# A sum of h split later on ScalarE, and two gate row copies moved to VectorE

## Chip, cores and metric

One core of one Trainium2 chip runs the whole program. The metric is the device time of one execution in microseconds, the median of three runs. TensorE does the matmuls, ScalarE (ACT) and VectorE (DVE) read their results and prepare their operands, SyncE (SP) and GpSimd (POOL) issue most of the transfers.

## What is computed

One decoder layer over 512 tokens of width 1024, in float32. What matters here is the head of it: the normalised input h is multiplied by the columns of one wide weight, in pieces.

```python
h = rmsnorm(x, norm_mix_g[i])
proj = h @ w_in[i]
qk_ml, v_ml, o_ml, if_pre, q_sw, k_sw, v_sw, g_a, g_b = jnp.split(proj, split_idx, axis=-1)
...
gates = (if_pre + b_if[i].astype(if_pre.dtype)).astype(jnp.float32)
ig = gates[..., :ML_HEADS]
lf = jax.nn.log_sigmoid(gates[..., ML_HEADS:])
h_ml = mlstm_chunkwise(q_ml, k_ml, v_ml.reshape(B, S, ML_HEADS, ML_DV), ig, lf)
```

Behind it come the mLSTM and the sliding-window attention, their two branch projections and the output projection, an MLP of width 4096, a gated per-layer embedding and a last norm.

## The kernel before

**Operands.** Every float32 operand of a product is split in a high part (rounded by ScalarE) and a low part (the rest, by VectorE), and each product takes three matmuls: high by high, high by low, low by high. `split` (L219) does so for a weight of 128x1024: the cast makes `wh`, the subtraction `wl`. There are four buffers of each (WB), and `load_w` (L243) is what loads and splits one. A weight that is loaded stands in `wr` or, from a scratch buffer, in `wq`.

**Seven products.** A projection over two halves of the tokens and two of the columns is done with seven block products in place of eight (`seven`, L646). These take, on the side of h, besides three blocks of h itself the four sums S1 to S4 of blocks; on the side of the weight they take the four blocks b11, b12, b21, b22, and sums of them that VectorE makes in place. Each block comes as two halves of 128x1024 in `by_tokens` (L711), and each half gives 12 matmuls of 512 columns. The products in order: p1 (A11), the one that ends in c11 (A12), u2 (S2 with the first form of b11), p5 (S1 with its second form), the one with S3, the one with S4 that ends in c12, and the one with A22.

**The sums of h.** S1 and S2 are made early. S3 and S4 are made in `late_sums` (L638), which `seven` calls in its first use (the v projection) behind the low part of b21. Each sum is split by `split_by_transfer` (L229): for each half a cast on ScalarE, a negated copy on ScalarE, and a transfer on POOL that adds the sum to that copy. So a sum costs four ScalarE instructions of 128x512 and two transfers; all of these write tiles named `hS`. The sums s1 to s4 lie in two scratch buffers of tag pT, which later hold weights of the gate projection b (`quads` of L269, named `wq`, loaded from in_w_gb by SP).

**The gates.** The pre-activations of the gates are turned into rows by eight small transposes into one bank pair, `pgi` and `pgf` (L763 to L767); behind the v projection the 4x512 rows are copied out as `ig` and `fg` (L777, L778), and `gates` (L799) works on them, beginning with `lf` on VectorE.

**Order.** In this part no order is written out by hand: instructions of an engine stand in a queue that is set when the program is built, by place in the program but with later work taken forward where earlier work isn't ready by the builder's own reckoning. `tc.issue_after(ins)` puts what is traced inside it, on the engine of `ins`, behind `ins`. Each engine runs its queue in order, and so does SP with its loads.

**Names.** `psa`, `pst`, `psg` are PSUM tiles; `p` is a product kept in SBUF and added to; `vm` and `vl` are the high and low part of v (L748), `vs` is a value of the attention, used far later (L1041).

Of the kernel before, what the change touches and what calls it, by code (L numbers as in the profile page):

```python
# [117 lines left out]
def block_kernel(  # L118
# [34 lines left out]
    V, A, G, T, L = [Turns(tc, e, fixed) for e in (nc.vector, nc.scalar, nc.gpsimd, nc.tensor, nc.sync)]  # L153
# [43 lines left out]
    def act_hl(n="s"):  # L197
        return [act_r(n), act_r(n)]
# [15 lines left out]
    def r32(t):  # L214
        return t.bitcast(F32)

    last_low = [None]

    def split(dst, src, scale=None):  # L219

        if scale is None:
            A.copy(dst[0], src)
            last_low[0] = V.tensor_sub(dst[1], src, r32(dst[0]))
        else:
            done = A.activation(dst[0], src, AF.Copy, scale=scale)
            V.scalar_tensor_tensor(dst[1], src, scale, r32(dst[0]), ALU.mult, ALU.subtract)
            return done

    def split_by_transfer(dst, src):  # L229

        A.copy(dst[0], src)
        A.activation(dst[1], src, AF.Copy, scale=-1.0)
        return nc.gpsimd.dma_start(out=r32(dst[1]), in_=src, accum_op=ALU.add)
# [9 lines left out]
    def load_w(src, n, dims, raw=None, cast=False, behind=None):  # L243

        if raw is None:
            raw = load_raw(src, n)
        parts = [wp.tile([P, 1024], F32R, tag=t, bufs=WB, name=nm(t))[:, :n] for t in ("wh", "wl")]
        if cast:
            nc.gpsimd.dma_start(out=parts[0], in_=src)
            with tc.issue_after(behind.ins) if behind else ExitStack():  # L250
                last_low[0] = V.tensor_sub(parts[1], raw[:, :n], r32(parts[0]))
        else:
            split(parts, raw[:, :n])
        return [q.rearrange("p (k c) -> p k c", k=dims) for q in parts]
# [317 lines left out]
    def hf_part(tok, par):  # L572

        return [hf[t + (2 if tok == 1 else 0)].rearrange("p (k two) c -> p k two c", two=2)[:, :, par - 1, :] for t in range(2)]
# [3 lines left out]
    def h_sum(name, a, b, op):  # L578
        t = sp.tile([P, 4, 256], F32, tag="pT", bufs=2, name=nm(name))
        halves = [t[:, :, :P], t[:, :, P:]]  # L580
        for i in range(2):
            V.tensor_tensor(halves[i], a[i], b[i], op)
        return t, halves
# [3 lines left out]
    def h_split(t):  # L587
        f = []
        for kh in range(2):
            hl = [q.rearrange("p (k c) -> p k c", k=2) for q in act_hl("hS")]  # L590
            summed[0] = split_by_transfer(hl, t[:, 2 * kh : 2 * kh + 2, :])
            f += [[q[:, k, :] for q in hl] for k in range(2)]
        return f
# [42 lines left out]
    S3, S4 = [], []  # L636

    def late_sums():  # L638
        s4, _ = h_sum("s4", hf_part(1, 2), s2h, ALU.subtract)
        s3, _ = h_sum("s3", hf_part(1, 1), hf_part(2, 1), ALU.subtract)  # L640
        S3.extend(h_split(s3))
        S4.extend(h_split(s4))

    ADDED = {"c11": "p1", "c22": "p5", "c12": "u2"}

    def seven(form, prod, X, Y, Z, b, post, own_first=False, sums_late=False, swapped=False, behind=None):  # L646

        b11, b12, b21, b22 = b  # L650
        n = range(len(b11))
        for i in n:
            prod(X, A11, form(b11[i]), i, True)
        post("p1", X)

        def weight_sums():
            for i in n:
                V.tensor_sub(b12[i], b22[i], b12[i])
                V.tensor_add(b11[i], b12[i], b11[i])

        if sums_late:
            w21 = [form(t) for t in b21]
            with tc.issue_after(last_low[0].ins):
                weight_sums()
        else:
            with tc.issue_after(behind.ins) if behind else ExitStack():
                weight_sums()
        for i in n:
            prod(Y, A12, w21[i] if sums_late else form(b21[i]), i, True, True)
        own = last_mm[0].ins  # L670
        if own_first:
            with tc.issue_after(last_low[0].ins):
                late_sums()
        post("c11", Y)
        for i in n:
            w = form(b11[i]) if sums_late else None
            with tc.issue_after(last_low[0].ins) if sums_late else ExitStack():
                V.tensor_sub(b21[i], b21[i], b11[i])
            w = w or form(b11[i])
            with tc.issue_after(own) if own_first else ExitStack():  # L680
                prod(X, S2, w, i, False)
            V.tensor_sub(b11[i], b22[i], b11[i])
        post("u2", X)
        if swapped:
            for i in n:
                prod(X, S3, form(b12[i]), i, False)
            post("u3", X)
        for i in n:
            prod(Z, S1, form(b11[i]), i, True)
        if swapped:  # L690
            post("c22", Z)
        else:
            post("p5", Z)
            for i in n:
                prod(X, S3, form(b12[i]), i, False)
            post("c22", X)
        rest = [("c12", Z, S4, b22), ("c21", X, A22, b21)]
        for what, ps, f, b in rest[::-1] if swapped else rest:
            for i in n:
                prod(ps, f, form(b[i]), i, False, True)  # L700
            post(what, ps)
# [9 lines left out]
    def by_tokens(w, post, own_first=False, sums_late=False):  # L711

        raws = quads(w, ["wr", "wr", "lm", "lm", "wr", "wr", "lm", "lm"])
        b = ps_a()
        X, Y, Z = [b[:, :512], b[:, 512:]], [ps_t(), ps_t()], [ps_g(), ps_g()]

        def prod(ps, f, w, kh, first, last=False):
            for t in range(2):
                ops = []
                for k in range(2):  # L720
                    ops += pairs([h[:, t * P : (t + 1) * P] for h in f[2 * kh + k]], [h[:, k, :] for h in w])
                chain(ps[t], ops, first and kh == 0, last and kh == 1, True)

        seven(lambda r: load_w(None, 1024, 2, r), prod, X, Y, Z, [raws[2 * i : 2 * i + 2] for i in range(4)], post, own_first, sums_late, behind=gate_in if own_first else None)
# [39 lines left out]
    pgi, pgf = pg[:, :512], pg[:, 512:]  # L764
# [7 lines left out]
    def row(n):  # L772
        return c1.tile([P, 512], F32, tag="row", bufs=NH, name=nm(n))

    ig = row("ig")[:4, :]
    fg = row("fg")[:4, :]
    A.copy(ig, pgi[:4, :])  # L777
    A.copy(fg, pgf[:4, :])  # L778
    god = dp.tile([P, NH, NT, DV], F32, name="god")

    def put_o(m, nh, ps, k):
# [64 lines left out]
    def by_features(blocks, tags, done, beside={}, swapped=False):  # L846
# [23 lines left out]
        def post(what, ps):  # L870
# [9 lines left out]
            for work in beside.pop(what, ()):  # L880
                work()

        seven(lambda r: load_w(None, 1024, 4, r), prod, X, Y, Z, [raws[i : i + 1] for i in range(4)], post, swapped=swapped, behind=added_last.get("c22") if swapped else None)

    def gate_proj(wd, beside={}):
# [129 lines left out]
    def swa_out(kp, ns):  # L1015

        terms = {n: swa_turn(kp, n) for n in ns}
        sums = {n: swa_sum(kp, terms[n]) for n in reversed(ns)}
        for n in ns:
            for g in range(4):  # L1020
                if n == 0:
                    yb[kp * 4 + g] = act_hl("yb")
                split([t[:, n * P : (n + 1) * P] for t in yb[kp * 4 + g]], sums[n][:, g * P : (g + 1) * P])
# [41 lines left out]
    def qk_parts(h):  # L1065
        for i in (h, 4 + h):
            hl = spare()
            split(hl, qk[i])
            qk[i] = hl
# [331 lines left out]
    A11, A22, A12, S3, S2, S1, S4 = range(7)  # L1401
# [48 lines left out]
    def form(user, dims, deps):  # L1450

        parts = []

        def high():
            parts.extend(wp.tile([P, 1024], F32R, tag=t, bufs=WB, name=nm(t)) for t in ("wh", "wl"))
            return [A.copy(parts[0], slots[user])]

        def low():
            return [V.tensor_sub(parts[1], slots[user], r32(parts[0]))]

        free = [forms[-WB]["use"]] if len(forms) >= WB else []
        h = plan.add("ACT", HI, high, deps + free + [w["hi"] for w in forms[-1:]])
        lo = plan.add("DVE", LO, low, [h] + free)
        w = {"hi": h, "lo": lo, "get": lambda: [q.rearrange("p (k c) -> p k c", k=dims) for q in parts]}
        forms.append(w)
        return w
# [618 lines left out]
```

## Time and profile before

| | |
|---|---|
| median of 3 runs | 859.73 us (859.72 to 860.01) |
| the profiled execution | 859.77 us |
| its span, first to last instruction | 858.0 us |
| TensorE matmuls busy | 848.6 us (99%) |
| VectorE busy | 722.4 us (84%) |
| ScalarE busy | 532.7 us (62%) |
| mean granted TensorE clock | 0.997 |

The profile is of one execution; its times run from the first instruction. Matmul records overlap, since they are pipelined, so the sum of the busy shares says less than the distance from one start to the next. Idle time of an engine counts only where TensorE waits in the end.

### The profile page before, as it was taken

How to read it: one execution, taken by the hardware profiler on the slowest of the kernel's cores; microseconds unless marked ns; L12 is line 12 of the kernel's file. 1: busy time of each engine (PE TensorE's matmuls, PEld its weight loads, DVE VectorE, ACT ScalarE, POOL GpSimd, SP SyncE). 2: the span in 40 equal slices, each digit the busy share in tenths (PEclk: the TensorE clock that was granted, in tenths of full speed). 3: DMA queues.
4: the chain of work that ended last, by engine and by line, in shares of the span. 5: the costliest groups of instructions: out<-in, count | busy, mean ns of one | idle time of the engine just before them, and what ended most of it. 6: DMA issues, size and time to landing. Idle time of an engine off the chain costs nothing.

```text
span 858.0 us, 12975 instructions
## 1 busy us (share of the span) xinstructions
PE 848.6 (99%) x4936; PEld 740.8 (86%) x4936; DVE 722.4 (84%) x1058; ACT 532.7 (62%) x923; POOL 59.3 (7%) x92
## 2 busy tenths in 40 slices
PE   9999999999999999999999999999999999999996
PEld 8878789999987778888888888899889989988886
DVE  6898979777799978777997799879988997999656
ACT  7786657556587758854353685458537744764743
POOL 2221111000000000000020000000000000010000
PEclk9999999999999999999999999999999999999998
DMA  7777235444421147468234271753455364634302
GB/s 294 216 190 283 91 131 199 148 147 147 149 73 50 50 138 254 167 221 297 104 61 133 96 226 49 217 133 117 98 173 147 113 178 130 170 102 134 134 1 99
DMA packets 37536, 125.71 MB, mean 147 GB/s; under 512 B 5213, under 2 KB 5213, under 8 KB 37474
## 3 DMA queue, kind: packets, MB, share of 16 engines
q1 hardware_dynamic: 28146, 95.77, 32.2%
q0 software_dynamic: 9184, 28.85, 13.9%
q8 instruction: 39, 0.64, 0.3%
q10 hardware_dynamic: 144, 0.26, 0.1%
q14 instruction: 23, 0.19, 0.1%
HBM read 106.51 MB, written 11.54 MB: 138 GB/s over the span
## 4 chain that ended last, share of the span: by engine, by line
PE 92%; DVE 5%; ACT 2%; issue 1%; DVEq 0%; ACTq 0%
PE psg L109 38%; PE psp L109 34%; PE psa L109 15%; PE pst L109 5%; DVE wl L109 1%; DVE wr L109 1%; ACT wh L109 1%; DVE wq L109 1%; DVE qs L109 1%; ACT hS L109 0%; ACT hf L109 0%; DVE s L109 0%; DVE kl L109 0%; DVE lm L109 0%; DVE pT L109 0%
## 5 line engine op out<-in xcount | busy, mean ns | idle before, releaser
L109 ACT CAST wh<-wr 128x1024 fp32r<-128x1024 f32 (+1 forms) x151 | 156.7, 1049 | 146.6 <-DVE wr L109 54.7
L109 DVE TENSOR_TENSOR wl<-wr,wh 128x1024 fp32r<-128x1024 f32 (+1 forms) x160 | 192.8, 1213 | 45.3 <-ACT wh L109 41.7
L109 PE MATMUL psp<-x,wh 128*128 128x256 f32 x672 | 121.3, 283 | 0.0
L109 PE MATMUL psp<-wh,uf 128*128 128x512 f32 x336 | 106.2, 390 | 0.0
L109 PEld LDWEIGHTS psp<-x,wh 128*128 128x128 f32 x672 | 105.0, 192 | 0.3
L109 PE MATMUL psp<-x,wl 128*128 128x256 f32 x336 | 95.1, 283 | 0.0
L109 PEld LDWEIGHTS psp<-wh,uf 128*128 128x128 f32 x336 | 63.1, 188 | 14.2 <-issue 1.2
L109 ACT CAST wh<-wd 128x1024 fp32r<-128x1024 f32 x45 | 47.2, 1049 | 33.0 <-PE psp L109 27.7
L109 PE MATMUL psp<-wl,uf 128*128 128x512 f32 x168 | 65.5, 390 | 0.0
L109 PEld LDWEIGHTS psp<-x,wl 128*128 128x128 f32 x336 | 64.5, 192 | 0.0
L109 PE MATMUL psg<-h,wh 128*128 128x512 f32 x192 | 60.9, 396 | 0.0
L109 DVE TENSOR_TENSOR wl<-wd,wh 128x1024 fp32r<-128x1024 f32 x45 | 54.7, 1218 | 3.1 <-ACT wh L109 3.1
L109 DVE TENSOR_TENSOR wr<-wr,wr 128x1024 f32<-128x1024 f32 x35 | 42.7, 1221 | 1.7 <-DMA wr<-in_w_gb 0.6
L109 PEld LDWEIGHTS psg<-h,wh 128*128 128x128 f32 x192 | 35.1, 188 | 9.0 <-issue 2.4
L109 DVE TENSOR_TENSOR uf<-F,uf 128x512 fp32r<-128x512 f32 (+3 forms) x36 | 34.9, 982 | 6.4 <-ACT uf L109 6.4
L109 PE MATMUL psg<-x,wh 128*128 128x512 f32 x128 | 39.5, 390 | 0.0
L109 PE MATMUL psg<-h,wl 128*128 128x512 f32 x96 | 37.7, 393 | 0.0
L109 PEld LDWEIGHTS psp<-wl,uf 128*128 128x128 f32 x168 | 31.5, 188 | 6.7 <-DVE wl L109 0.3
L109 PE MATMUL psg<-wh,uf 128*128 128x512 f32 x112 | 36.5, 389 | 0.0
L109 ACT CAST uf<-F 128x512 fp32r<-128x512 f32 (+3 forms) x36 | 30.7, 856 | 7.5 <-DVE F L109 7.1
L109 PE MATMUL psg<-ya,wh 128*128 128x512 f32 x112 | 34.8, 391 | 0.0
L109 DVE SCALAR_TENSOR_TENSOR xk<-psp,r,xk 128x512 f32<-128x512 f32 x42 | 30.4, 745 | 4.8 <-PE psp L109 4.7
(355 smaller groups left out, 2090.0 us busy)
## 6 DMA issues: line engine op xcount, KB each, us to landing
wr<-in_w_down SPq DMA_DIRECT2D x16, 512.0 KB, 4.7
wd<-in_w_down SPq DMA_DIRECT2D x16, 512.0 KB, 4.3
wr<-in_w_upb SPq DMA_DIRECT2D x12, 512.0 KB, 4.0
wd<-in_w_upb SPq DMA_DIRECT2D x12, 512.0 KB, 4.6
gd<-gr POOLq DMA_DIRECT2D x8, 512.0 KB, 3.0
wr<-in_w_qkml SPq DMA_DIRECT2D x8, 512.0 KB, 3.3
wr<-in_w_b SPq DMA_DIRECT2D x8, 512.0 KB, 3.4
wh<-in_w_b POOLq DMA_DIRECT2D x8, 512.0 KB, 3.9
```

Of the source, the lines that this page charges most:

```text
L109: ins = op(*args, **kw)
```

## The change

Three things are done. `split` keeps the last cast it issued. `late_sums` makes s3 and s4 and splits s3 as before, but hands s4 back; `seven` splits s4 behind its loop over u2, and on ScalarE behind the last cast issued there, which is the one of the second half of b11. And the two copies of gate rows are issued by VectorE.

```diff
@@ split
-    last_low = [None]
+    last_low, last_cast = [None], [None]
...
         if scale is None:
-            A.copy(dst[0], src)
+            last_cast[0] = A.copy(dst[0], src)
             last_low[0] = V.tensor_sub(dst[1], src, r32(dst[0]))
@@ late_sums
         S3.extend(h_split(s3))
-        S4.extend(h_split(s4))
+        return s4
@@ seven
         if own_first:
             with tc.issue_after(last_low[0].ins):
-                late_sums()
+                s4 = late_sums()
         post("c11", Y)
...
             V.tensor_sub(b11[i], b22[i], b11[i])
+        if own_first:
+            with tc.issue_after(last_cast[0].ins):
+                S4.extend(h_split(s4))
         post("u2", X)
@@ behind the v projection
-    A.copy(ig, pgi[:4, :])
-    A.copy(fg, pgf[:4, :])
+    V.tensor_copy(ig, pgi[:4, :])
+    V.tensor_copy(fg, pgf[:4, :])
```

## Rows read from the trace of the kernel before

**Rows 1.** The page: busy time and share of each engine; the last chain by engine.
```profile
PE 848.6 (99%) x4936; PEld 740.8 (86%) x4936; DVE 722.4 (84%) x1058; ACT 532.7 (62%) x923; POOL 59.3 (7%) x92
...
PE 92%; DVE 5%; ACT 2%; issue 1%; DVEq 0%; ACTq 0%
```

**Rows 2.** Waits of TensorE's matmuls, whole span: who for whom, us, times, longest.
```profile
PE psg L109 <- DVE zero L109: 1.1, 1, 1.1
PE psa L109 <- DVE wl L109: 0.5, 1, 0.5
```

**Rows 3.** Windows: stretch, length, busy us of each engine, clock, DMA share, GB/s.
```profile
56.75:63.03 6.28, 5.78 (x26) 4.43 (x24) 5.61 (x7) 6.25 (x9) 3.20 (x4) 1.00 1.06 205
63.03:68.60 5.57, 5.57 (x25) 4.42 (x24) 4.64 (x5) 5.54 (x8) 0.00 (x0) 1.00 0.98 338
68.60:74.04 5.44, 5.44 (x25) 4.50 (x24) 4.60 (x8) 3.48 (x5) 0.00 (x0) 1.00 1.00 393
```

**Rows 4.** Timeline of TensorE's weight loads, 56 to 66: start, us, what, idle before.
```profile
60.36 0.19 PEld L109 LDWEIGHTS psa<-wl,hS 128*128 128x128 f32 x1 [0.92 <-DVE wl L109]
...
63.23 0.19 PEld L109 LDWEIGHTS psg<-wl,hS 128*128 128x128 f32 x1 [0.24 <-DVE wl L109]
```

**Rows 5.** Timeline of ScalarE, 46 to 60.
```profile
46.52 0.57 ACT L109 COPY ig<-psa 4x512 f32<-4x512 f32 x1
...
48.65 0.58 ACT L109 CAST qs<-psg 64x512 fp32r<-64x512 f32 x1 [1.09 <-DVE qs L109]
...
53.31 0.63 ACT L109 CAST hS<-s 128x512 fp32r<-128x512 f32 x1
...
55.40 0.62 ACT L109 CAST hS<-s 128x512 fp32r<-128x512 f32 x1
...
57.48 0.62 ACT L109 CAST vm<-p 128x512 fp32r<-128x512 f32 x1
57.99 1.05 ACT L109 CAST wh<-wr 128x1024 fp32r<-128x1024 f32 x1
...
59.47 1.05 ACT L109 CAST wh<-wr 128x1024 fp32r<-128x1024 f32 x1
```

**Rows 6.** Timeline of VectorE, 55 to 63.
```profile
55.32 0.67 DVE L109 SCALAR_TENSOR_TENSOR lf<-fg 4x512 f32<-4x512 f32 x1
55.92 0.41 DVE L109 TENSOR_TENSOR vs<-vs,vs 128x256 f32<-128x256 f32 x1
56.35 1.36 DVE L109 TENSOR_TENSOR p<-pst,p 128x512 f32<-128x512 f32 x2
58.13 0.69 DVE L109 TENSOR_TENSOR vl<-p,vm 128x512 fp32r<-128x512 f32 x1 [0.42 <-ACT vm L109]
59.08 1.23 DVE L109 TENSOR_TENSOR wl<-wr,wh 128x1024 fp32r<-128x1024 f32 x1 [0.25 <-ACT wh L109]
...
60.82 1.22 DVE L109 TENSOR_TENSOR wr<-wq,wr 128x1024 f32<-128x1024 f32 x1
61.96 1.22 DVE L109 TENSOR_TENSOR wl<-wr,wh 128x1024 fp32r<-128x1024 f32 x1
```

**Rows 7.** Waits of SP's queue, 40 to 90.
```profile
SPq L276 <- DMA hS<-s: 12.0, 2, 9.6
```

**Rows 8.** The tile wq, 40 to 90: durations in ns, first and last start.
```profile
L276 SPq DMA_DIRECT2D wq<-in_w_gb x2: 333/334/334, 59.7 to 62.6; - x2
```

**Rows 9.** Timelines of SP, TensorE and ScalarE, 63 to 78.
```profile
63.20 1.81 SPq L276 DMA_DIRECT2D wr<-in_w_o x2
...
74.04 0.39 PE L109 MATMUL psg<-wh,hS 128*128 128x512 f32 x1
...
77.00 1.05 ACT L109 CAST wh<-wr 128x1024 fp32r<-128x1024 f32 x1 [0.67 <-ACT vm L109]
```

**Rows 10.** The tile hS: its transfers from issue to landing.
```profile
DMA to landing us min/median/max: 3.2/4.0/6.5
```

**Rows 11.** The tile gc: the copies from PSUM on VectorE, durations in ns.
```profile
L109 DVE COPY gc<-pst x5: 154/160/161, 150.7 to 151.0; 128x16 f32<-128x16 f32 x2, 128x4 f32<-128x4 f32 x1, 128x8 f32<-128x8 f32 x1, 128x12 f32<-128x12 f32 x1
```

## The prediction

> **What bounds the kernel now.** I read four views, from wide to narrow. First the busy times and the chain that ended last: TensorE matmuls fill 99% of the span and 92% of the chain [rows 1], so an edit on ScalarE or VectorE can only matter where TensorE waits for one of them. Second, TensorE's own waits, the whole span through: beside 1.1 us at the very start there is one of any size, 0.5 us in a product into psa for a low weight part `wl` written by VectorE [rows 2]. Third, the stretch around that wait: from 56.75 to 68.60 TensorE runs the 24 matmuls of u2 and the 24 of p5 of the first seven products (the v projection). The 24 matmuls of the next product take 5.44 us [rows 3]; those of u2 take 6.28 and those of p5 5.57. So the stretch loses 0.84 + 0.13 = **0.97 us**, and that is all that this change can win near its place. The granted clock is 1.00 in all three windows, the upper of the two levels (2.4 GHz), so no clock is to be won. Fourth, what TensorE was late for: the weight load of u2's second half waits 0.92 us and that of p5's first half 0.24 us, both for a `wl` of VectorE [rows 4].
>
> Why are these late? ScalarE runs the eight instructions of the third and fourth sum of h (hS) back to back from 53.31; those of the fourth begin at 55.40, then comes one `vm`, and only at 57.99 the rounding `wh` of u2's second half [rows 5]. VectorE can make its `wl` from 59.08 on, and it ends at 60.31 [rows 6]. The `wl` of p5's first half has another cause: its `wh` starts at 59.47 and takes 1.05, so it is there at 60.52 [rows 5], but VectorE comes to it only at 61.96, behind `vl` and the sum of a weight (wr from wq and wr, at 60.82) [rows 6]. So the first wait is ScalarE's queue, the second VectorE's own queue.
>
> **The change part by part.** Part one, the four instructions of the fourth sum go behind the cast `wh` of u2's second half. The third sum still runs 53.31 to 55.40. The cast then takes 55.40 to 56.45 instead of 57.99 to 59.04 [rows 5]: 2.6 us sooner, 2.1 by the four instructions and 0.5 by the `vm`, which isn't ready at 55.40, since its `p` is added on VectorE from 56.35 on [rows 6]. ScalarE's work until the next cast (p5's first half) is the same sum in another order, so that cast still ends near 60.5.
>
> What is moved with the fourth sum: its two transfers on POOL and what waits for them. Four instructions from 56.45 end at 58.5, where they now end near 57.5, so the last transfer is issued about 1.0 us later. The load of a weight of the next stage but one (in_w_gb) into the scratch buffer that the sum frees is issued on SP at 62.6, after SP waited 12.0 us in two waits for such transfers [rows 7, 8]; behind it in SP's queue stand the loads of w_o, the first at 63.20 [rows 9]. They go perhaps 0.5 us later, and ScalarE first rounds a piece of w_o at 77.00, 13.8 us after that issue [rows 9]: free. TensorE reads the fourth sum from 74.04 on [rows 9]; issued near 59 and with a landing of at most 6.5 us [rows 10] it is there by 65.5: free as well, by 8.5 us. Were that cover gone, each us late would be a us of TensorE.
>
> Part two, the two copies of gate rows. On ScalarE they take 0.57 us each, two in a row from 46.52 on (the first stands in the rows), and behind them ScalarE idles 1.09 us for VectorE's `qs` [rows 5]: taking them out gives nothing. On VectorE they are new. No row shows a 4x512 copy from PSUM there. Below it lies the small copy from PSUM, 0.16 us for 4 to 16 columns [rows 11]; above it the 4x512 operation with one tensor, 0.67 us [rows 6]. I take 0.60, the start-to-start distance of that operation and the next (55.32 to 55.92), since the width is equal. So VectorE gets 2 x 0.60 = **1.20 us** more (0.32 to 1.34), in the very stretch in which it makes the two late `wl`. As the rows of their consumer show (`lf` at 55.32 and `vs` at 55.92, both far later in the program, run in a hole ahead of `p`), work that nobody needs soon goes where VectorE would wait. I expect the copies in that same hole, since `lf` depends on one of them, and `lf` and `vs` (55.32 to 56.35, 1.03 us) [rows 6] pushed out of it, behind the weights.
>
> The Trainium skill speaks against part two: Perfetto Trace Analysis, section Optimizing Scalar/DVE Operations, gives about 125 ns of access overhead for DVE on PSUM against 51 ns for Scalar, and advises to move work from a saturated DVE to Scalar, not the other way. By its two figures the move costs an estimated 2 x 0.07 = 0.15 us of engine time more than it saves; the rows agree on the load (VectorE 5.61 busy of 6.28 us in u2's window [rows 3]), and the rule's result is the second rival below.
>
> The sum on VectorE from 55.32: copies to 56.52, two `p` (1.36, by starts 1.28) to 57.80, `wl` of u2 1.2 to **59.00**. TensorE would load it at 60.36 - 0.92 = 59.44: no wait, 0.84 us won. Next two `vl` of 0.6 to 60.20, the weight sum 1.14 to 61.34, `wl` of p5's first half 1.2 to **62.54** (its `wh` is there at 60.5). In the kernel before, the load was free for it at 63.23 - 0.24 = 62.99, and it waited 0.24 for a loss of 0.13 [rows 3, 4]; with TensorE 0.84 sooner it is free at 62.15, waits 0.39, and loses some 0.1 less than that, 0.3. Left of 0.97: 0.3; won: about **0.65 us**. After 68.60 all that VectorE and ScalarE do is released by TensorE or has us of room, so nothing is given back that I can see. The profiled execution took 859.77 (span 858.0 and 1.77 around it), 0.04 over the median of the three runs: 859.77 - 0.65 = **859.1**.
>
> **The rivals.** First, all 0.97 goes, if `vl` too falls behind the `wl` of p5 or a copy costs near 0.16: 859.77 - 0.97 = 858.8. For it: the `vl` has until the v heads are read, far later. Against it: in the rows one `vl` stands ahead of each of these `wl`.
>
> Second, and slower: VectorE becomes the bound. If `lf` and `vs` keep their place ahead of `p`, all of VectorE's line above is 1.03 us later: `wl` of u2 ends 60.03 (0.6 late, some 0.5 lost), that of p5 at 63.57. TensorE, free at 62.15 without any wait, then loads 1.42 us late and loses 1.3 in all: 0.3 more than the 0.97 of now, 860.1; with copies of 0.67, 860.25. It decides from the point where that `wl` ends after 63.2, its end now. For it: VectorE has but 0.42 + 0.25 us of idle in that stretch [rows 6], less than the 1.20 it is given. Against it: `lf` and `vs` aren't needed soon, and it only takes one of them to leave for the time to fall under that of before.
>
> Third, the change doesn't do what it says: the first `vm` stays ahead of the moved cast in ScalarE's queue. Its `p` ends near 57.2, `vm` 57.7, the cast 58.75, `wl` at best 59.95: 0.5 late in place of 0.92, and p5 as forecast or worse: 859.4 to 859.8.
>
> Fourth, the fourth sum comes too late: it is queued behind the casts up to 70 us instead of right behind the one it is tied to. Then it lands after 74, and TensorE stands still for us: 862 and more. Against it: in program order it stands ahead of all of p5's casts.
>
> **How the numbers follow.** Forecast (0.3 to 0.9 won, 858.9 to 859.5) 0.47; first rival 0.1 (858.8); second 0.25 (859.6 to 860.3); third 0.08; fourth 0.04 (over 862); and 0.06 for queue orders that move elsewhere, 0.03 of it faster and 0.02 slower by more than 0.2%. 0.2% of 859.7 is 1.7 us, about what a measurement of this kernel can tell from no change; the whole stretch is worth 0.97. So faster by more than 0.2% only with queues that move elsewhere, 0.03; slower with these or the fourth rival, 0.06; within, 0.91. The range takes in the forecast, the first three rivals and their bounds: 858.7 to 860.3.
>
> **What would show it.** Right: no wait of TensorE for `wl` near 59.5, the cast of u2's second half right behind the third sum on ScalarE, u2's 24 matmuls in about 5.45 us; p5's in 5.6 to 5.9; the two copies on VectorE between 55 and 57 with some 0.6 each, `lf` behind `p`; in_w_gb's second load about 1 us later with nothing behind it late. Wrong: u2 still over 6 us (third rival, or the second), p5 over 6.3 us (second), TensorE waiting for hS near 74 (fourth), or the loss gone here and back at a later `wl`, which would show as a new wait for VectorE between 68 and 100.

## The result

The changed kernel takes 861.15 us (860.13 to 862.11, 22 runs) where the kernel before takes 859.73 (859.04 to 860.20): a ratio of 1.0016, 95% interval 1.0010 to 1.0023. That is 1.4 us slower, within the 0.2% that were called no change, but outside the range of 858.7 to 860.3, and on the other side of the forecast of 859.1. Its runs also spread over 2.0 us, those of before over 1.2.

What TensorE does at the place of the change came as forecast. Its timeline in the changed kernel, the first matmuls of u2, of p5 and of the product with S3:

```profile
56.64 0.39 PE L109 MATMUL psa<-wh,hS 128*128 128x512 f32 x1
...
62.08 0.39 PE L109 MATMUL psg<-wh,hS 128*128 128x512 f32 x1
...
67.82 0.39 PE L109 MATMUL psa<-wh,hS 128*128 128x512 f32 x1
```

u2 takes 5.44 us and not 6.28, p5 5.74 and not 5.57 [rows 3]: 11.18 for both in place of 11.85, so 0.67 us are won. VectorE has the copies where they were expected, and `lf` later:

```profile
55.31 0.68 DVE L109 COPY ig<-psa 4x512 f32<-4x512 f32 x1
55.92 0.67 DVE L109 COPY fg<-psa 4x512 f32<-4x512 f32 x1
...
62.32 0.67 DVE L109 SCALAR_TENSOR_TENSOR lf<-fg 4x512 f32<-4x512 f32 x1
```

But later there are new waits. TensorE's waits in the changed kernel (who for whom, us in total, times, longest), against [rows 2]:

```profile
PE psa L109 <- DVE wl L109: 2.4, 2, 1.6
```

and the weight loads that waited, in the stretch from 80 to 104 us, which is the o projection; the kernel before has one such wait there, of 0.48 us:

```profile
95.30 0.19 PEld L109 LDWEIGHTS psa<-wh,hS 128*128 128x128 f32 x1 [0.55 <-ACT wh L109]
96.56 0.19 PEld L109 LDWEIGHTS psa<-wl,hS 128*128 128x128 f32 x1 [1.07 <-DVE wl L109]
101.16 0.19 PEld L109 LDWEIGHTS psa<-wl,hS 128*128 128x128 f32 x1 [2.03 <-DVE wl L109]
```

VectorE and ScalarE are late there because of loads. ScalarE's timeline has it, the casts of the second half of w_o, first in the kernel before, where they wait for no load, then in the changed kernel:

```profile
82.44 1.06 ACT L109 CAST wh<-wr 128x1024 fp32r<-128x1024 f32 x1 [0.63 <-ACT vm L109]
...
85.60 1.05 ACT L109 CAST wh<-wr 128x1024 fp32r<-128x1024 f32 x1
```

```profile
85.18 1.05 ACT L109 CAST wh<-wr 128x1024 fp32r<-128x1024 f32 x1 [3.59 <-DMA wr<-in_w_o]
...
87.32 1.05 ACT L109 CAST wh<-wr 128x1024 fp32r<-128x1024 f32 x1 [0.60 <-DMA wr<-in_w_o]
```

And SP's timeline has where the loads were held:

```profile
59.54 0.33 SPq L276 DMA_DIRECT2D wq<-in_w_gb  x1
62.46 2.37 SPq L276 DMA_DIRECT2D wr<-in_w_o  x2
72.41 0.33 SPq L276 DMA_DIRECT2D wq<-in_w_gb  x1
72.83 1.91 SPq L276 DMA_DIRECT2D wq<-in_w_o  x4
74.83 2.32 SPq L276 DMA_DIRECT2D wr<-in_w_o  x2
```

The second load of in_w_gb goes at 72.41, not at 62.6 [rows 8], and the six loads of w_o behind it in SP's queue go from 72.83 on, where the first of them went at 66.58 before. (Before, all eight loads of w_o stood behind both loads of in_w_gb [rows 8, 9]; when the changed kernel was built, two of them came to stand ahead of the second one.) SP's waits from 40 to 110 name what it waited for, the transfers of the sums, 17.3 us in place of 12.0 [rows 7]:

```profile
SPq L276 <- DMA hS<-s: 17.3, 2, 9.9
```

The landings show how this makes the casts late. The two loads into `wr` at the end of that list, which the late casts read, were hardly held themselves: they go at 74.83 and near 76.8, and in the kernel before at 73.86 and 76.69. But now four other loads of w_o, of 512 KB each, go between 72.83 and 74.83, just ahead of them. The issues of these two from 73 to 78 (KB each, median us to landing), first in the kernel before, then in the changed kernel:

```profile
wr<-in_w_o SPq DMA_DIRECT2D x2, 512.0 KB, 4.5
```

```profile
wr<-in_w_o SPq DMA_DIRECT2D x2, 512.0 KB, 10.3
```

The chain that ended last, from 82 to 104 us of the changed kernel, begins with the first of the two and leads to the load at 101.16:

```profile
74.83 10.26 DMA wr<-in_w_o
```

The fourth sum reached that point late twice over. ScalarE's and POOL's timelines:

```profile
55.28 1.99 ACT L109 CAST wh<-wr 128x1024 fp32r<-128x1024 f32 x2
57.22 0.62 ACT L109 CAST vm<-p 128x512 fp32r<-128x512 f32 x1
59.56 0.62 ACT L109 CAST vm<-p 128x512 fp32r<-128x512 f32 x1 [1.71 <-DVE p L109]
60.08 0.62 ACT L109 CAST hS<-s 128x512 fp32r<-128x512 f32 x1
...
61.55 0.75 POOL L748 DMA_DIRECT2D vld<-vl  x1 [1.58 <-DVE vl L109]
62.30 1.81 POOL L233 DMA_DIRECT2D hS<-s  x2
```

Its first instruction starts at 60.08 and not at 56.45, behind two casts and two `vm` and an idle time of 1.71 us for the second `p`; and from the first POOL issue of the sum at 62.30 to SP's load at 72.41 pass 10.1 us. Its two transfers took 7.5 and 9.4 us to land, where [rows 10] had 6.5 as the longest.

### The profile page after: what moved, and what is told of

It is laid out like the page before. It is cut to its first block, busy times and chain, and to the rows that moved or that the text cites. A ratio compares the mean times of both kernels' runs of the same rounds, so it can differ in the third digit from the quotient of the medians.

```text
span 860.2 us, 12974 instructions
## 1 busy us (share of the span) xinstructions
PE 848.7 (99%) x4936; PEld 740.6 (86%) x4936; DVE 723.1 (84%) x1060; ACT 531.7 (62%) x921; POOL 59.5 (7%) x92
## 4 chain that ended last, share of the span: by engine, by line
PE 91%; DVE 4%; ACT 2%; DMA 1%; issue 1%; DVEq 0%; ACTq 0%
PE psg L109 36%; PE psp L109 34%; PE psa L109 15%; PE pst L109 6%; DMA wr<-in_w_o 1%; ACT wh L109 1%; DVE wl L109 1%; DVE lm L109 1%; DVE qs L109 0%; DVE wr L109 0%; ACT lm L109 0%; DVE mx L109 0%; DVE wq L109 0%; ACT xn L109 0%; ACT L109 0%
```

## Experiments

Two theories stood at first. A: SP's queue, as just read. B: VectorE, which got 1.2 us more and makes the weight sums and low parts for which TensorE waits at 96 and 101 us. The medians below stand beside the kernel before on the same chip: 859.51 in the first four, 859.65 in the second four.

### The two in_w_gb loads behind w_o's (e1)

```diff
+            with tc.issue_after(gb_behind[0].ins) if tags[i] == "pT" and gb_behind[0] else ExitStack():
+                quad_load[0] = nc.sync.dma_start(out=raw, in_=src[i])
...
     by_tokens(w_o, post_by_tokens(put_o), sums_late=True)
+    gb_behind[0] = quad_load[0]
```

> The changed kernel, but the two loads of in_w_gb into the scratch buffers of the sums stand behind the loads of w_o in SP's queue. The queues of ScalarE and VectorE are the same as in the changed kernel. Theory A (SP's queue: the second in_w_gb load waits for the fourth sum's transfer, and six loads of w_o wait behind it): w_o's loads go when their buffers are free, TensorE's waits at 96 and 101 us are gone, u2 stays without a wait: 858.8 to 859.3, some 2 us under the changed kernel. Theory B (VectorE: 1.2 us of copies make its weight sums and low parts of the w_o stage late): the queues of VectorE are the same, so the waits at 96 and 101 stay: 860.8 to 861.5.

Measured: 859.08 us, ratio to before 0.9995 (0.9986 to 1.0004). SP's timeline, and the one weight load that still waits for VectorE between 85 and 101:

```profile
62.66 2.37 SPq L277 DMA_DIRECT2D wr<-in_w_o  x2
66.61 6.07 SPq L277 DMA_DIRECT2D wq<-in_w_o  x4
73.48 0.33 SPq L277 DMA_DIRECT2D wr<-in_w_o  x1
73.91 0.37 SPq L277 DMA_DIRECT2D wq<-in_w_gb  x1
...
98.31 0.19 PEld L109 LDWEIGHTS psa<-wl,hS 128*128 128x128 f32 x1 [0.43 <-DVE wl L109]
```

ScalarE's and VectorE's queues are those of the changed kernel, the copies on VectorE among them, and the waits of the changed kernel are gone; the one at 98.31 is that of the kernel before (0.48 us there). The two late loads into `wr`, which go at 73.48 and 77.03 here, land in 4.9 and 7.2 us in place of 10.3 and 10.4. Theory B falls, and A holds: what costs is w_o's place behind the second in_w_gb load. The time is 0.43 us under that of the kernel before, less than the interval can tell from no change. The last load to wait stands at 101.16 in the changed kernel and at 98.31 here; with the 0.20 us by which this profile is later at u2's end (62.65 against 62.45 for the same load) the block cost 101.16 + 0.20 - 98.31 = 3.05 us in that execution.

### The same move in the kernel before (e7)

The edit of e1 on the kernel before.

> The kernel before with the two in_w_gb loads behind w_o's loads in SP's queue and nothing else: what the move of these loads does by itself. Theory A: w_o has no lateness to lose, the waits of u2 and p5 stay: 859.3 to 859.9, no change. If it were faster by itself by 0.4 or more, the gain of the first run of this study would be that of the load order, not of the block that it takes away.

Measured: 859.59 us, ratio 0.9998 (0.9989 to 1.0007). The order of these loads gives nothing by itself; e1 takes away a cost of the change.

### The copies alone (e2)

```diff
-    A.copy(ig, pgi[:4, :])
-    A.copy(fg, pgf[:4, :])
+    V.tensor_copy(ig, pgi[:4, :])
+    V.tensor_copy(fg, pgf[:4, :])
```

> The kernel before with the two gate row copies on VectorE alone; the fourth sum is split where it was. Theory A: SP's queue is as before, w_o is there in time; only u2 and p5 can get later by VectorE's 1.2 us: 859.5 to 860.3, no wait between 85 and 101. Theory B: the waits near 96 and 101 are there, u2's too: 861 to 862.5.

Measured: 859.31 us, ratio 0.9998 (0.9989 to 1.0007). The weight loads of u2 and p5 that wait, against [rows 4]:

```profile
60.22 0.19 PEld L109 LDWEIGHTS psa<-wl,hS 128*128 128x128 f32 x1 [0.39 <-DVE wl L109]
63.70 0.19 PEld L109 LDWEIGHTS psg<-wl,hS 128*128 128x128 f32 x1 [0.61 <-DVE wl L109]
```

The waits at 96 and 101 of the changed kernel aren't there. The 24 matmuls of u2 take 5.74 us in place of 6.28 and those of p5 5.94 in place of 5.57, so the stretch is 0.17 us shorter with VectorE's 1.2 us more, and by itself this edit costs no time. But it isn't the price of two copies alone, since ScalarE's queue changed with them: the cast of u2's second half now stands ahead of both `vm`, where one stood ahead of it before [rows 5].

```profile
57.87 1.04 ACT L109 CAST wh<-wr 128x1024 fp32r<-128x1024 f32 x1
58.81 1.14 ACT L109 CAST vm<-p 128x512 fp32r<-128x512 f32 x2
```

This profile is 0.38 us later than that of the kernel before (53.69 against 53.31 at the third sum). With that taken off, the `wl` for which p5 waits comes only 0.09 later than before (63.70 - 0.38 - 63.23); the rest of p5's longer wait is TensorE coming sooner out of u2.

### The fourth sum alone (e3)

The changed kernel with the copies back on ScalarE.

> The changed kernel with the two gate row copies back on ScalarE, so the fourth sum alone is moved. In ScalarE's queue it now also stands behind the two gate activations with their table loads, so it comes some 3 us later than in the changed kernel. Theory A: the second in_w_gb load goes at 72 or later, w_o late again: 861 to 863, waits near 96 and 101. Theory B: no copies on VectorE, no such waits, u2's 0.8 us won: 858.8 to 859.3.

Measured: 860.36 us, ratio 1.0009 (1.0000 to 1.0018): 0.85 us slower by the medians, with an interval that just reaches no change. Both theories missed. The second in_w_gb load goes at 68.96, and TensorE waits no longer near 96 and 101 than before. The loss is at p5: u2 takes 5.44 us, but p5 7.05, 12.49 for both in place of 11.85. ScalarE's timeline, and the weight loads that wait:

```profile
57.21 1.28 ACT L109 ACT_TABLE_LOAD   x1
...
59.67 1.28 ACT L109 ACT_TABLE_LOAD   x1
...
61.50 0.60 ACT L109 CAST hS<-s 128x512 fp32r<-128x512 f32 x1
...
63.58 1.03 ACT L109 CAST wh<-wr 128x1024 fp32r<-128x1024 f32 x1
...
64.66 0.19 PEld L109 LDWEIGHTS psg<-wh,hS 128*128 128x128 f32 x1 [0.72 <-ACT wh L109]
65.92 0.19 PEld L109 LDWEIGHTS psg<-wl,hS 128*128 128x128 f32 x1 [1.07 <-DVE wl L109]
```

With the copies made early on ScalarE, `lf` is ready early, and both gate activations with their table loads come ahead of the fourth sum and of the cast of p5's second half, which is then late for TensorE. So at p5 the two parts of the change belong together: with the copies on VectorE, `lf` is made at 62.32 and the first table load comes at 67.52. In the time as a whole this kernel is still under the changed one (860.36 against 861.15, on two chips). Its fourth sum starts later, at 61.50, and its transfers are issued at 62.94 and 64.24, but they land in 4.4 and 4.6 us, so in_w_gb goes 3.5 us sooner than in the changed kernel. The two w_o loads ahead of it go at 61.59 and 65.90 here, at 62.46 and 64.49 there.

### Only the transfers late (e4)

The kernel before, with the fourth sum's two POOL transfers behind the second store of v's low part:

```diff
+        if own_first:
+            store_low()
+            with tc.issue_after(stored[0].ins):
+                for go in s4_add:
+                    go()
```

> The kernel before, ScalarE's split of the fourth sum where it was and the copies on ScalarE; only the two POOL transfers that add the fourth sum are put behind the second store of v's low part, as in the changed kernel (from about 62 us). Theory A: the second in_w_gb load waits for them, w_o late as in the changed kernel, and u2's 0.97 us isn't won: 861.5 to 863. Theory B: VectorE and ScalarE as before: 859.6 to 860.0.

Measured: 859.40 us, ratio 0.9997 (0.9989 to 1.0006). Theory A was wrong in its size: SP's queue has the order of the changed kernel and is held here too, and it costs nothing.

```profile
69.83 0.33 SPq L279 DMA_DIRECT2D wq<-in_w_gb  x1
70.25 2.02 SPq L279 DMA_DIRECT2D wq<-in_w_o  x4
73.42 3.16 SPq L279 DMA_DIRECT2D wr<-in_w_o  x2
```

(SP's timeline.) The load at 69.83 is 7.2 us later than in the kernel before and free; at 72.41 it is 2.6 us later still and costs some 3. So the queue had at least 7.2 us of room here. Not much was left: the first of the two loads into `wr` lands in 8.5 us, at 81.9, and its cast starts at 82.00.

### The order that the prediction assumed (e5)

```diff
-        post("c11", Y)
+        if not own_first:
+            post("c11", Y)
...
                 S4.extend(h_split(s4))
+            with tc.issue_after(last_neg[0].ins):
+                post("c11", Y)
...
-            prod(Z, S1, form(b11[i]), i, True)
+            with tc.issue_after(last_neg[0].ins) if own_first else ExitStack():
+                w = form(b11[i])
+            prod(Z, S1, w, i, True)
```

Here `last_neg` is the last negated copy of the fourth sum on ScalarE.

> The changed kernel with the order that the prediction assumed: ScalarE splits the fourth sum right behind the cast of u2's second half, ahead of the two vm and of p5's casts (post of c11 is issued behind it). SP's queue has both in_w_gb loads ahead of w_o again. Theory A (what costs is when the fourth sum's transfers land, since SP's queue waits for it): they are issued near 57 to 59, ahead of w_o's loads, and land in 4 to 6.5 us; the second in_w_gb load goes near 64, no wait of TensorE for wl at 96 or 101, u2 without a wait: 858.9 to 859.4. Theory C (the order of ScalarE's and VectorE's work around the moved sum costs it): p5 waits by more than 1 us or the waits at 96 and 101 stay: 860.5 or more.

Measured: 858.90 us, ratio 0.9991 (0.9982 to 1.0000), the lowest median of all that were run, with an interval that just reaches no change. Timelines of ScalarE, POOL and SP:

```profile
55.42 1.05 ACT L109 CAST wh<-wr 128x1024 fp32r<-128x1024 f32 x1
56.35 0.63 ACT L109 CAST hS<-s 128x512 fp32r<-128x512 f32 x1
...
58.04 1.70 POOL L233 DMA_DIRECT2D hS<-s  x2 [1.37 <-ACT hS L109]
...
59.68 5.57 SPq L277 DMA_DIRECT2D wq<-in_w_gb  x2
65.36 0.84 SPq L277 DMA_DIRECT2D wr<-in_w_o  x2
```

The fourth sum starts at 56.35, the prediction had 56.45; w_o's loads follow from 65.36 on, and TensorE waits nowhere in u2 or p5. u2 and p5 take 5.44 us each, so the whole 0.97 us is won there, as in the first rival and not as in the forecast: one of the two `vl` falls behind p5's `wl`. By the medians 0.75 us are won, inside the range of the forecast (0.3 to 0.9 won); that measurement doesn't tell 0.65 from 0.97. What it shows is that with the fourth sum in the place that the prediction assumed, the loads of w_o aren't late, and the loss is gone.

### w_o's loads behind the transfer (e6)

```diff
+    probe = dp.tile([P, 8], F32, name="probe")
+    landed = L.dma_start(out=probe, in_=r32(S4[3][1])[:, :8])
+    with tc.issue_after(landed.ins):
+        by_tokens(w_o, post_by_tokens(put_o), sums_late=True)
```

> The changed kernel, but all loads of w_o wait in SP's queue for the landing of the fourth sum's last transfer (a load of 8 columns reads its result first), and the second in_w_gb load is behind them. So no load of w_o is under way while that transfer is. In the changed kernel the transfer took 9.4 us with two w_o loads under way. Theory A1 (the two loads slow the transfer): it lands in 4 to 6 us, by 68, w_o's eight loads follow, the last near 82 to 84: 858.9 to 859.8. Theory A2 (the transfer takes its 9 us anyway): it lands at 72, eight loads behind it: the last near 87, waits at 96 and 101: 861 to 863.

Measured: 859.22 us, ratio 0.9994 (0.9985 to 1.0003). The transfers' issues from 61 to 70 us (KB each, median us to landing), first here, then in the changed kernel:

```profile
hS<-s POOLq DMA_DIRECT2D x2, 256.0 KB, 4.7
```

```profile
wr<-in_w_o SPq DMA_DIRECT2D x2, 512.0 KB, 6.1
hS<-s POOLq DMA_DIRECT2D x2, 256.0 KB, 8.4
```

The transfers are issued at nearly the same time (62.09 and 62.30). With no load of w_o under way they land in 4.4 and 5.0 us, with two of them in 7.5 and 9.4. So theory A1: the loads slow the very transfer for which SP waits in front of the next loads. The Trainium skill says so in general: in DMA: Bandwidth & Descriptors, section Issuing engines are not separate DMA queues, what is issued from the scalar, sync or gpsimd engine runs on the same 16 DMA engines and interleaves; the two rows agree.

### The changed kernel again (e8)

> The changed kernel itself, beside the three others on the same chip, and a second profile of it. Theory A: 860.2 to 862; the second in_w_gb load again near 70 to 73 us, and the time is the longer the later it is. Theory B: the same time, with the waits at 96 and 101 of the same size whatever the load's time.

Measured: 860.92 us (860.15 to 862.17), ratio 1.0014 (1.0005 to 1.0023). The profiled execution took 860.37, the first one 861.97. SP's timeline and the weight load that waits:

```profile
72.01 0.33 SPq L276 DMA_DIRECT2D wq<-in_w_gb  x1
...
99.51 0.19 PEld L109 LDWEIGHTS psa<-wl,hS 128*128 128x128 f32 x1 [2.02 <-DVE wl L109]
```

The load goes 0.40 us sooner, and of the three waits one is left: 99.51 + 0.38 (this profile is so much earlier at p5 than that of e1) - 98.31 = 1.6 us lost in place of 3.05. That is about 1.5 of the 1.60 us between the two executions. So the load's time isn't all: 0.40 us sooner goes with some 1.5 less lost. What follows it differs as well: the two last loads into `wr` landed in 9.0 and 9.2 us here, in 10.3 and 10.4 there. With two executions, that the spread of the changed kernel's runs is the spread of these landings is likely, but not shown.

## Why the prediction was wrong

**The bound and the local gain were right.** TensorE's two waits had the causes named, the copies stood at 55.31 and 55.92 on VectorE in the hole of `lf` and `vs`, some 0.6 apart, the `lf` went behind, u2's wait was gone, and of 0.97 us p5 kept 0.30. Forecast won: 0.65; measured 0.67. VectorE's order was not that of the forecast (`wl` of u2 at 57.12, between the two `p`), but the same work stands ahead of p5's `wl`, so the sum for it holds.

**The step that failed is "They go perhaps 0.5 us later, and ScalarE first rounds a piece of w_o at 77.00, 13.8 us after that issue [rows 9]: free."** With it falls "nothing is given back that I can see" for all that comes after 68.60: about 3 us were, in the profiled execution. The step named the right queue and the right wait, and sized it wrongly, in three terms. First, the start of the fourth sum on ScalarE: 60.08 and not 56.45, since behind a cast is not right behind it. p5's cast (expected to end near 60.5, ended at 57.27) and both `vm` were put between, and the second `vm` had to wait for its `p`, which VectorE made only at 58.85, behind the `wl` of u2 and the first `vl`. The prediction had this in hand, for the `vm` in its third rival and for the casts in its fourth, but priced neither for SP's queue. Second, the landing: 6.5 us was taken as a ceiling from transfers of the kernel before; the later issue put it among w_o's first two loads, where it took up to 9.4 (e6 against the changed kernel shows the cause). This term weighs more than the first: in e3 the sum starts later still, and SP's queue is held less. Third, the cover: 13.8 us were read off the first piece of w_o, which wasn't held at all in the end. The pieces behind the in_w_gb load are the other six, and the last two of these are what came late (casts at 85.18 and 87.32). For these the hold counted by what it put beside them: they were issued at 74.83 and near 76.8, about as before, but right behind four loads that had waited for in_w_gb, and landed in over 10 us in place of 4.1 and 4.8. A hold of 7.2 us was still free in e4, 9.8 were not. That the bunched loads slow each other is read from these traces side by side; no run moves the last two alone.

**The rivals.** The first and the second, on VectorE, didn't come. e2 agrees with what was said against the second: `lf` kept a place between the two `p`, `vs` left it, and the time did not rise. The Trainium skill's rule behind the second rival (Perfetto Trace Analysis, section Optimizing Scalar/DVE Operations: spare a saturated DVE) is right on the direction of the price, 0.68 and 0.67 us a copy in place of 0.57. But here the two waits for VectorE got no longer in sum (e2), and e3 shows that at p5 the copies on ScalarE cost more, by what they let start early. The fourth rival had the fourth sum late for TensorE at 74, with a point far off; the true one was late for SP's queue, and decides some us earlier. It had no chance of its own but for a part of the 0.06 for queues that move elsewhere. The last sign of being wrong, the loss back as a new wait for a `wl` of VectorE between 68 and 100, is the one that came, at 96.56, with a larger one at 101.16.

**What would have told it** in the rows of before: SP's 62.6 is the end of a wait with all loads of w_o behind it [rows 7 to 9], and the last of those loads, not the first, have the least room: they land at 78.0 and 81.5 and are rounded at 82.44 and 85.60, some 4 us later.

## What to carry to other kernels

When a step is moved later, follow every buffer that it frees to the queue that waits for it, and count the room at the last load in that queue that matters, not the first, up to its landing: loads that were held go together and land later. To put work behind an instruction doesn't put it next: if the place matters, tie what might slip in between as well (e5 does, and has 0.75 us less than the kernel before on its chip, where the changed kernel has 1.3 more). And take the landing time of a moved transfer from the traffic of its new place.

## What had not been expected of the hardware

Adding transfers of 256 KB from POOL landed in 4.4 and 5.0 us with no load of w_o under way (e6) and in 7.5 and 9.4 with two such loads of 512 KB from SP beside them, issued 2.0 us apart at the same point of the changed kernel. With the two loads 4.3 us apart (e3) they landed in 4.4 and 4.6.
